# Six buffers for raw weights instead of four, and 42 places for activations instead of 46, in a two-layer hybrid decoder

## Chip, cores and metric

The kernel runs on one core of a Trainium2 chip. Its time is that of one execution on the device, in microseconds (us), and the median of several runs counts. TensorE (PE) does the matmuls, VectorE (DVE), ScalarE (ACT) and GpSimd (POOL) the work on elements, and SyncE (SP) issues most transfers (DMAs) from HBM to the on-chip memory.

## What is computed

Two layers of a decoder over 256 tokens of width 1024, in float32. Each layer has a shift, scale and gate from a vector c (adaLN), an input projection, three token mixers side by side, a merge, an output projection with a norm, and a feed-forward part with a short convolution. Cut to that:

```python
for l in range(DEPTH):
    mod = jax.nn.silu(c) @ mod_w[l] + mod_b[l]
    sh1, sc1, gt1, sh2, sc2, gt2 = jnp.split(mod[:, None, :], 6, axis=-1)
    h = x * (1.0 + sc1) + sh1
    z = h @ w_in[l]                       # layer 1: 32 more columns
    xa, ga, q, k, v, zc, zgate = _split(z, IN_SPLITS)
    y_a = _rg_lru(_causal_dwconv(xa, ...), ...) * jax.nn.gelu(ga)       # branch A
    y_b = _dilated_attention(rope(q), rope(k), v)                       # branch B
    y_c, v_first = _rwkv7_branch(_token_shift(zc, rwkv_mu[l]), ...)     # branch C
    g_a, g_b, g_c = jnp.split(jax.nn.sigmoid(zgate), N_BRANCH, axis=-1)
    merged = g_a * (y_a @ proj_a[l]) + g_b * (y_b @ proj_b[l]) + g_c * (y_c @ proj_c[l])
    x = _layer_norm(ALPHA * x + (1.0 + gt1) * (merged @ w_o[l]), ln1_w[l], ln1_b[l])
    h = x * (1.0 + sc2) + sh2
    u_g, u_v = jnp.split(_causal_dwconv(h @ ffn_up[l], ...), 2, axis=-1)
    x = _layer_norm(ALPHA * x + (1.0 + gt2) * ((jax.nn.silu(u_g) * u_v) @ ffn_down[l]), ln2_w[l], ln2_b[l])
```

## The kernel before

Channels lie on the partitions and tokens along the free axis. Every large product is made of three matmuls of a reduced-precision float32 type (fp32r): a weight is split in a high part `whi` (a rounded copy) and a low part `wlo` (the raw weight minus `whi`), an activation in the same way (`hh` and `hl` for the layer's input), and high times high, high times low and low times high are added up in PSUM. A weight item is one 128x1024 block, 512 KB, with 24 matmuls of 256 columns.

**The weights' path.** All weights pass in one list, `items`, in the order of their use. An item is loaded by SP to a raw buffer `w32` (the trace calls it `w`) from a ring of `NW` buffers. ACT or POOL then makes `whi` in two halves, and DVE or POOL `wlo` in two halves; `whi` and `wlo` have `WB` = 4 buffers each. The raw buffer is free again when the second `wlo` half is done. Between the weights stand the items of the modulation ("mods"): a column block of mod_w, which DVE multiplies by silu(c) and sums up, without PE; it needs a raw buffer and nothing else. In the feed-forward stage of the first layer the mods have a small ring of their own, of tiles `wc` in the activations' pool.

The loads are issued in this loop (`w_dma`), which the planner calls again and again; `wring` holds the items in the ring, and an item stands in `raw` until its `wlo` (or its reduction) has been written into the program:

```python
ring, room = (cring, NSC) if i in apart else (wring, NW)
old = ring[-room] if len(ring) >= room else None
if old in raw:
    return
```

So a load comes into SP's queue when the item `NW` places before it has been worked off by the program's order. On the chip the load waits until that work is done, and all loads behind it on SP wait with it.

**The start.** The first 16 mods make shift and scale of layer 0. Two of them, then the six weights of the first group (split to `ehi` and `elo`, in the activations' pool), and then the other 14 mods, with the four parts of x between them. Each pair of mods gives one of eight blocks of the layer's input: POOL and ACT make `h` and `hh`, DVE makes `hl`, and PE multiplies that block by all six weights (18 matmuls).

**What sets the order.** The order in which instructions stand on each engine is made when the program is built, by the class `Flow`. It keeps a clock per engine and for the loads, takes the dense matmuls as the main stream, and puts the steps of the branches, the mods and the splits between them by estimated times. It also chooses the engine of a split (`pick`, `pick_hi`). `NW` comes into it, since an item's arrival is worked out from the time at which its buffer is free. The engines then run their own queues in order and wait for each other by semaphores.

**The activations' pool.** Nearly all tiles of 128x512 float32 share one tag, `s2`, with `NS2` places of 2 KB per partition. A new tile takes a place whose tile has been released; the first write then waits for the last use of the old one. In branch C the recurrence over four chunks uses `KB`, `AL`, `AR`, `UV` and others of this pool, and writes the small tiles `R`, `UV` and `Y` on ACT step by step; branch A uses `rr`, `ii` and `tt`.

Of the kernel before, what the change touches and what calls it, by code (L numbers as in the profile page):

```python
# [50 lines left out]
DEBUG = None  # L51
WB = 4
TRACE = None
NW = 4
NG = 6
NSC = 2
NS2 = 46
NT1 = 21
HOLD = 0.3
BIAS_HI = 1.1  # L60
# [261 lines left out]
def hybrid_kernel(ctx: ExitStack, tc: tile.TileContext, x, c, positions, mod_w, w_in, w_qkv, w_vres, lru, lora, g2w,  # L322
# [22 lines left out]
    def s2(shape, name, dtype=F32):  # L345
        return sb.tile(shape, dtype, name=name, tag="s2", bufs=NS2)

# [25 lines left out]
    def fetch(dst, src, dep=0.0):  # L373

        nc.sync.dma_start(dst, src)
        n = dst.shape[0] / 128
        for d in dst.shape[1:]:
            n *= d
        fl.t["DMA"] = max(fl.t["DMA"], max(dep, fl.t["PE"]) + 1.1) + 0.00163 * n
        return fl.t["DMA"] + 1.0  # L380
# [20 lines left out]
    def w_dma():  # L401
        while state["dma"] < len(items):
            i = state["dma"]
            src, n, _, first = items[i]
            ring, room = (cring, NSC) if i in apart else (wring, NW)
            old = ring[-room] if len(ring) >= room else None
# [9 lines left out]
            else:  # L416
                raw[i] = wp.tile([128, 1024], F32, name="w32", bufs=NW)
                arrive[i] = fetch(raw[i][:, :n], src, dep)
# [1528 lines left out]
```

## Time and profile before

| | us |
|---|---|
| median of 3 runs | 1405.0 (1403.71 to 1406.58) |
| the profiled execution | 1404.2 |
| its span | 1402.5 |
| PE busy in it | 1322.6 |
| DVE busy | 1106.0 |
| ACT busy | 852.3 |
| POOL busy | 284.3 |

The span runs from the first to the last instruction of the profiled execution; the 1.7 us beside it are the ends of the launch. An engine's busy time counts its instructions, not its waits. Behind a row, the brackets name what ended the idle time before it. Matmuls are pipelined, so that their rows overlap.

### The profile page before, as it was taken

How to read it: one execution, taken by the hardware profiler on the slowest of the kernel's cores; microseconds unless marked ns; L12 is line 12 of the kernel's file. 1: busy time of each engine (PE TensorE's matmuls, PEld its weight loads, DVE VectorE, ACT ScalarE, POOL GpSimd, SP SyncE). 2: the span in 40 equal slices, each digit the busy share in tenths (PEclk: the TensorE clock that was granted, in tenths of full speed). 3: DMA queues.
4: the chain of work that ended last, by engine and by line, in shares of the span. 5: the costliest groups of instructions: out<-in, count | busy, mean ns of one | idle time of the engine just before them, and what ended most of it. 6: DMA issues, size and time to landing. Idle time of an engine off the chain costs nothing.

```text
span 1402.5 us, 32614 instructions
## 1 busy us (share of the span) xinstructions
PE 1322.6 (94%) x12798; PEld 1250.0 (89%) x12798; DVE 1106.0 (79%) x2547; ACT 852.3 (61%) x1755; POOL 284.3 (20%) x459
## 2 busy tenths in 40 slices
PE   4889999988999999999999999999999999999996
PEld 3789888887899999999999998988889899999996
DVE  7798778788668779999968748787788687799954
ACT  3546686666775557665457666755868454667643
POOL 2304141213200031110040321523205000510001
PEclk9999999989999999999999999999999999999998
DMA  8745435334447646778945443462435546267662
GB/s 307 247 148 181 129 95 189 117 123 136 152 144 248 209 166 209 243 256 293 328 159 181 137 127 111 150 212 92 152 107 191 181 150 226 94 226 240 195 188 66
DMA packets 77613, 249.21 MB, mean 178 GB/s; under 512 B 8754, under 2 KB 12082, under 8 KB 77460
## 3 DMA queue, kind: packets, MB, share of 16 engines
q1 hardware_dynamic: 76660, 244.62, 53.1%
q0 software_dynamic: 800, 2.52, 0.5%
q8 instruction: 100, 1.64, 0.5%
q14 instruction: 53, 0.43, 0.1%
HBM read 243.96 MB, written 3.15 MB: 176 GB/s over the span
## 4 chain that ended last, share of the span: by engine, by line
PE 58%; DVE 23%; ACT 9%; DMA 6%; issue 4%; POOL 0%; SPq 0%; DVEq 0%; ACTq 0%; POOLq 0%
PE mm L270 43%; PE aux L270 8%; DVE wlo L270 7%; PE faux L270 6%; DMA w<-in_w_in_dram 2%; DVE w L270 2%; ACT whi L270 2%; DVE u L270 2%; DVE xc L270 1%; DVE wc L270 1%; DVE BK L270 1%; DMA w<-in_w_up_dram 1%; DMA w<-in_mod_w_dram 1%; ACT L270 1%; DVE sq L270 1%
## 5 line engine op out<-in xcount | busy, mean ns | idle before, releaser
L270 PE MATMUL mm<-hh,whi 128*128 128x256 f32 x1696 | 499.5, 294 | 0.0
L270 ACT ACTIVATE whi<-w 128x512 fp32r<-128x512 f32 (+1 forms) x652 | 373.4, 617 | 200.4 <-PE mm L270 61.2
L270 PE MATMUL mm<-hh,wlo 128*128 128x256 f32 x1696 | 482.3, 284 | 7.3 <-DVE wlo L270 7.1
L270 PE MATMUL mm<-hl,whi 128*128 128x256 f32 x1696 | 480.9, 284 | 0.0
L270 DVE TENSOR_TENSOR wlo<-w,whi 128x512 fp32r<-128x512 f32 (+1 forms) x630 | 414.9, 695 | 50.4 <-ACT whi L270 47.2
L270 PEld LDWEIGHTS mm<-hh,whi 128*128 128x128 f32 x1696 | 321.4, 190 | 12.3 <-issue 4.3
L270 PEld LDWEIGHTS mm<-hh,wlo 128*128 128x128 f32 x1696 | 322.1, 190 | 10.9 <-DVE wlo L270 10.4
L270 PEld LDWEIGHTS mm<-hl,whi 128*128 128x128 f32 x1696 | 322.2, 190 | 1.1
L270 POOL TENSOR_TENSOR wlo<-w,whi 128x512 fp32r<-128x512 f32 x72 | 99.4, 1384 | 350.7 <-ACT whi L270 262.9
L270 POOL TENSOR_SCALAR whi<-w 128x512 fp32r<-128x512 f32 x50 | 33.5, 674 | 332.6 <-PE mm L270 258.6
L270 PE MATMUL mm<-fal,whi 128*128 128x256 f32 x352 | 98.8, 281 | 1.3 <-DVE fal L270 1.3
L270 PE MATMUL mm<-fah,wlo 128*128 128x256 f32 x352 | 99.1, 281 | 0.2 <-DVE wlo L270 0.2
L270 PE MATMUL mm<-fah,whi 128*128 128x256 f32 x352 | 99.0, 281 | 0.1
L270 DVE SCALAR_TENSOR_TENSOR u<-mm,par,u 128x255 f32<-128x255 f32 (+1 forms) x172 | 82.3, 479 | 14.0 <-ACT u L270 10.9
L270 PE MATMUL mm<-wlo,hh 128*128 128x256 f32 x288 | 82.4, 286 | 2.7 <-DVE wlo L270 2.7
L270 PE MATMUL mm<-whi,hh 128*128 128x256 f32 x288 | 83.9, 291 | 0.0
L270 PE MATMUL mm<-whi,hl 128*128 128x256 f32 x288 | 82.1, 285 | 0.0
L270 DVE SCALAR_TENSOR_TENSOR w<-w,s_bc 128x512 f32<-128x512 f32 x96 | 70.4, 756 | 0.5 <-DMA w<-in_mod_w_dram 0.4
L270 PEld LDWEIGHTS mm<-fal,whi 128*128 128x128 f32 x352 | 66.2, 188 | 1.6 <-DVE fal L270 1.5
L270 PEld LDWEIGHTS mm<-fah,wlo 128*128 128x128 f32 x352 | 66.2, 188 | 0.7 <-DVE wlo L270 0.6
L270 PEld LDWEIGHTS mm<-fah,whi 128*128 128x128 f32 x352 | 66.3, 188 | 0.3 <-ACT fah L270 0.3
L270 ACT ACTIVATE u<-mm,par 128x256 f32<-128x256 f32 x86 | 47.6, 556 | 28.7 <-PE mm L270 28.7
(446 smaller groups left out, 2728.8 us busy)
## 6 DMA issues: line engine op xcount, KB each, us to landing
w<-in_w_in_dram SPq DMA_DIRECT2D x132, 512.0 KB, 3.6
w<-in_w_up_dram SPq DMA_DIRECT2D x88, 512.0 KB, 4.4
w<-in_mod_w_dram SPq DMA_DIRECT2D x64, 512.0 KB, 4.5
w<-in_w_qkv_dram SPq DMA_DIRECT2D x36, 512.0 KB, 3.4
wc<-in_mod_w_dram SPq DMA_DIRECT2D x64, 256.0 KB, 5.0
w<-in_w_dn_dram SPq DMA_DIRECT2D x32, 512.0 KB, 4.6
w<-in_w_pa_dram SPq DMA_DIRECT2D x16, 512.0 KB, 4.3
w<-in_w_pc_dram SPq DMA_DIRECT2D x16, 512.0 KB, 3.8
```

The source lines that it names most:

```text
L270: r = f(*a, **k)
```

## The change

Two numbers change. The ring of raw weights gets two more buffers (2 x 4 KB per partition), and the activations' pool four places fewer (4 x 2 KB).

```diff
 WB = 4
 TRACE = None
-NW = 4
+NW = 6
 NG = 6
 NSC = 2
-NS2 = 46
+NS2 = 42
 NT1 = 21
```

Since the planner works with `NW`, the order on the engines is a new one from about 45 us on; ahead of that it is the same on every engine. The number of loads is unchanged.

On POOL, around 300 us, where PE multiplies the gate weights and the first weights of branch A. `itmp` and `VS` are steps of a small inverse in branch C; `w_3915` is the raw buffer of one weight item, and so on. Before:

```order
L270 TENSOR_TENSOR VS<-VS,itmp 128x7x2
L270 TENSOR_TENSOR itmp<-VS,N_3523 128x8
L270 TENSOR_TENSOR VS<-VS,itmp 128x8
L270 TENSOR_TENSOR wlo<-w_3915,whi 128x512
L270 TENSOR_SCALAR whi<-w_4182 128x512
L270 TENSOR_TENSOR wlo<-w_4182,whi 128x512 x2
```

Now:

```order
L270 TENSOR_TENSOR VS<-VS,itmp 128x7x2
L270 TENSOR_SCALAR whi<-w_3850 128x512
L270 TENSOR_TENSOR itmp<-VS,N_3544 128x8
L270 TENSOR_TENSOR VS<-VS,itmp 128x8
L270 TENSOR_SCALAR whi<-w_3850 128x512
L270 TENSOR_SCALAR whi<-w_3897 128x512
L270 TENSOR_TENSOR wlo<-w_3850,whi 128x512 x2
L270 TENSOR_TENSOR wlo<-w_3897,whi 128x512
L270 TENSOR_TENSOR wlo<-w_3972,whi 128x512
L270 TENSOR_TENSOR wlo<-w_3991,whi 128x512
L270 TENSOR_SCALAR whi<-w_4033 128x512
L270 TENSOR_TENSOR wlo<-w_3991,whi 128x512
```

On POOL stand now four halves of `whi` and seven of `wlo` (the last of them one row below these) for the items 3850 to 4033.

On ACT, around 956 us (layer 1), where branch C's recurrence of one pair of heads and branch A run side by side. `D_`, `N` and `VS` belong to the next pair of heads. Before:

```order
L270 ACTIVATE UV_11967<-aux 64x128
L270 ACTIVATE rr<-faux,h_ba_824 128x256
L270 ACTIVATE ii<-faux,h_bx_826 128x256
L270 ACTIVATE tt<-rr,sp_1119 128x256
L270 ACTIVATE Y<-aux 128x2x64
L270 ACTIVATE xc<-mm,par_84 128x256
L270 ACTIVATE whi<-w_12968 128x512
L270 ACTIVATE R<-aux 128x128
L270 ACTIVATE D__13221<-AL_13117 32x256
L270 ACTIVATE D__13221<-AL_13118 32x256
L270 ACTIVATE N_13230<-NP,pf 128x256
L270 ACTIVATE VS<-eye_153 128x128
```

Now:

```order
L270 ACTIVATE UV_11972<-aux 64x128
L270 ACTIVATE D__13200<-AL_13074 32x256
L270 ACTIVATE D__13200<-AL_13075 32x256
L270 ACTIVATE N_13209<-NP,pf 128x256
L270 ACTIVATE VS<-eye_153 128x128
L270 ACTIVATE rr<-faux,h_ba_854 128x256
L270 ACTIVATE ii<-faux,h_bx_856 128x256
L270 ACTIVATE tt<-rr,sp_1233 128x256
L270 ACTIVATE Y<-aux 128x2x64
L270 ACTIVATE xc<-mm,par_84 128x256
L270 ACTIVATE whi<-w_12863 128x512 x2
L270 ACTIVATE R<-aux 128x128
```

Branch A's `rr`, `ii` and `tt` have moved behind the next pair's `D_`, `N` and `VS`. With 42 places `ii` and `tt` take those of the pair `KB_12313` and `KB_12314`, two operands of the recurrence.

## Rows read from the trace of the kernel before

**Rows 1.** The page, parts 1 and 2: busy us (share) xinstructions; granted clock in tenths.

```profile
PE 1322.6 (94%) x12798; PEld 1250.0 (89%) x12798; DVE 1106.0 (79%) x2547; ACT 852.3 (61%) x1755; POOL 284.3 (20%) x459
...
PEclk9999999989999999999999999999999999999998
```

**Rows 2.** Stretches: us, busy PE, PEld, DVE, ACT, POOL (instructions); clock, DMA share, GB/s.

```profile
0.00:45.00 45.00, 20.74 (x114) 17.03 (x115) 34.99 (x93) 13.78 (x23) 9.94 (x22) 1.00 0.89 318
45.00:112.00 67.00, 59.36 (x452) 55.32 (x453) 57.23 (x184) 41.59 (x82) 16.84 (x32) 0.92 0.51 167
210.00:350.00 140.00, 126.48 (x1490) 115.80 (x1490) 113.92 (x244) 88.49 (x195) 33.54 (x62) 0.94 0.42 140
```

**Rows 3.** The chain that ended last, one step: start us, us, engine, instructions.

```profile
407.09 50.37 PE mm L270 x426
```

**Rows 4.** PE's waits in the whole run: us in total, times, longest us.

```profile
PE mm L270 <- DVE hl L270: 17.4, 5, 12.2
PE mm L270 <- DVE wlo L270: 9.9, 14, 3.2
```

**Rows 5.** SP's queue in the start, by the timeline: start us, us.

```profile
2.86 10.55 SPq L375 DMA_DIRECT2D w<-in_w_in_dram  x6
```

**Rows 6.** DVE in the first 46 us: two waits, and the first mod (timeline).

```profile
DVE w L270 <- DMA w<-in_mod_w_dram: 4.1, 7, 0.9
DVE elo L270 <- ACT ehi L270: 2.9, 4, 1.5
...
7.05 1.28 DVE L270 CUSTOM_DVE_ANT_0 w<-w,s_bc,modb 128x1024 f32<-128x1024 f32 x1 [0.93 <-DMA w<-in_mod_w_dram]
```

**Rows 7.** DMA, 0 to 42 us in 40 slices; loads to landing; a stretch as rows 2.

```profile
GB/s 0 2 127 195 291 417 417 410 425 417 320 332 164 285 281 289 226 378 412 421 373 300 316 316 359 258 341 404 425 390 328 328 224 275 417 394 339 254 285 324
...
w<-in_mod_w_dram SPq DMA_DIRECT2D x16, 512.0 KB, 5.4
...
28.80:45.80 17.00, 11.89 (x93) 11.07 (x93) 14.14 (x33) 3.21 (x6) 3.39 (x5) 1.00 0.95 354
```

**Rows 8.** PE's waits for `wlo`, and ACT's loads before two of them (timeline).

```profile
79.37 0.39 PE L270 MATMUL mm<-wlo,hh 128*128 128x256 f32 x1 [0.69 <-DVE wlo L270]
88.19 0.39 PE L270 MATMUL mm<-wlo,hh 128*128 128x256 f32 x1 [1.97 <-DVE wlo L270]
1253.65 0.39 PE L270 MATMUL mm<-hh,wlo 128*128 128x256 f32 x1 [1.64 <-DVE wlo L270]
...
78.08 1.15 ACT L270 ACTIVATE whi<-w 128x512 fp32r<-128x512 f32 x2 [1.02 <-DMA w<-in_w_qkv_dram]
1249.29 1.15 ACT L270 ACTIVATE whi<-w 128x512 fp32r<-128x512 f32 x2 [1.35 <-DMA w<-in_w_up_dram]
```

**Rows 9.** Branch A's `tt` and the last reads of `KB` and `AL` (timeline).

```profile
956.40 0.59 ACT L270 ACTIVATE tt<-rr,sp 128x256 f32<-128x256 f32 x1
956.52 0.46 PE L270 MATMUL aux<-UV,KB 128*64 128x64 f32 x8
961.64 0.28 PE L270 MATMUL aux<-UV,AL 64*64 64x64 f32 x2
```

**Rows 10.** Around 303 us: PE, DVE and POOL (timeline), and a stretch as rows 2.

```profile
306.19 0.58 PE L270 MATMUL mm<-hh,wlo 128*128 128x256 f32 x1 [3.23 <-DVE wlo L270]
301.13 1.78 DVE L270 SCALAR_TENSOR_TENSOR w<-w,s_bc 128x512 f32<-128x512 f32 x1
302.84 0.68 DVE L270 SCALAR_TENSOR_TENSOR w<-w,s_bc 128x512 f32<-128x512 f32 x1
301.06 1.31 POOL L270 TENSOR_TENSOR wlo<-w,whi 128x512 fp32r<-128x512 f32 x1 [14.96 <-ACT whi L270]
305.30:312.10 6.80, 5.91 (x85) 5.62 (x86) 6.55 (x16) 3.50 (x8) 0.00 (x0) 0.50 0.39 134
```

**Rows 11.** The page, part 5: POOL's splits, busy, mean ns, idle before.

```profile
L270 POOL TENSOR_TENSOR wlo<-w,whi 128x512 fp32r<-128x512 f32 x72 | 99.4, 1384 | 350.7 <-ACT whi L270 262.9
L270 POOL TENSOR_SCALAR whi<-w 128x512 fp32r<-128x512 f32 x50 | 33.5, 674 | 332.6 <-PE mm L270 258.6
```

## Prediction

> **What bounds the kernel now.** I read the page's engine table and slices first: TensorE (PE) is busy 94% of the span at a granted clock near full, so only PE's gaps and its half-clock stretches can be won [rows 1]. The busy times by stage tell where the gaps are: 24 of PE's 80 idle us lie in the first 45 us, 7.6 in the next 67, 13.5 between 210 and 350 [rows 2]. Where PE is fed it runs unbroken, 426 matmuls in 50.4 us, 0.118 us each; one weight item is 24 of them, 2.83 us [rows 3]. PE's list of waits tells for whom it stands: 17.4 us in all for `hl`, the low half of the first layer's input, all in the first 45 us, and 9.9 us in 14 waits for `wlo`, the low half of a weight [rows 4]. Only these two lie behind the raw buffers. The rest of the gaps are the serial steps of the recurrence (branch C) and the norms, which no raw buffer feeds.
>
> In the first 45 us the chain is: load, VectorE's (DVE) reduction of a modulation column, `hl`, PE. The DMA issues show the ring of four: once it is full the issuing queue stands until a buffer is free, so that six weights are spread over 10.55 us [rows 5]. DVE waits meanwhile: 4.1 us for loads of mods in seven waits (0.9 of it before the first load can be there) and 2.9 us for `ehi`, whose ScalarE (ACT) step waits for a weight's load [rows 6].
>
> **The change, term by term.** The sum is made against the profiled execution, 1404.2 us; the median of the runs shown, 1405.0, is 0.8 above it, and I add that at the end.
>
> *Start.* The items, their order and their instructions up to about 45 us are the same; only the buffer that each load waits for is two items older. Upper end: all of DVE's waits of [rows 6] but the very first go, 3.2 + 2.9 = 6.1 us. A round of one buffer is 5.4 us to landing [rows 7] and 1.4 us of reduction, 6.8 us; four buffers give an item each 1.7 us, six each 1.13 us, while DVE itself needs 1.54 us per mod (1.28 [rows 6], 0.08 to read the sum out, and half of a 0.34 us `hl`). So with six DVE sets the pace. Lower end: the DMA engines. From 28.8 to 45.8 us they were busy 0.95 at 354 GB/s [rows 7], which would be 373 GB/s when never idle. The single us from 10 to 16 show 320, 332, 164, 285, 281, 289 and 226 GB/s, mean 271, although 410 to 425 went through in the us 5 to 9 [rows 7]; filled up to 373, these seven us give 1.9 us, the stretch from 18 to 28.8 (mean 345) 0.8, the rest 0.9: 3.6 us. If the engines have nothing to give past the last 5%, 0.9. I take 4.0, near the 3.6, since DVE's pace (1.18 MB per pair of mods with its part of `x`, in 3.08 us, 383 GB/s) is just above what 373 feeds. PE then waits for `hl` less by as much; the steps behind it start from `hl` too and move along.
>
> The Trainium skill, page "DMA: Bandwidth & Descriptors", section Specifications, gives some 358 GB/s as the limit of HBM for one core, and that speaks against this term. By it the start would win 2.3 us (1.7, 0.4 and 0.2 in the three stretches) and the time would come to 1401. The trace has 410 to 425 GB/s in five us on end, so I don't take it as a ceiling.
>
> *Weights later on.* PE's waits for `wlo` whose ACT step waited for a load: 1.64 us at 1253.65, where ACT had stood 1.35 us for a load of w_up, and 0.69 us at 79.37 behind 1.02 us for a load of w_qkv [rows 8]. A load that is issued two items (5.7 us of PE) earlier is there. That is 2.3 us. Lower end 0 (the planner's order is new at both places), upper end 4.7: of the 9.9 us all but the 3.2 and 2.0 before which DVE, not a load, was late [rows 8, 10]. What is in it beyond 2.3 are ten small waits with no load just ahead of them. I take 2.3, the two with one.
>
> *The activations' pool, 42 places.* At 956.4 us branch A's `tt` is written, and counting tiles from first write to last read in the trace it is the 43rd in use; `NP` at 963.7 is one again. In the new order `ii` and `tt` get the places of the `KB` pair (the order of ACT there is shown above). Of before, `KB` was read last by matmuls from 956.52 for 0.46 us; the next tiles to be released there are the `AL`, read until 961.9 [rows 9]. So ACT is held 0.6 us, or 5.5 us if `AL` is what it waits for. I take 0.6, because `KB` stands there by name. Queued behind it on ACT are a `Y`, an `R` and the next `whi`; PE's recurrence waits for `R`, so nothing hides a long hold. At all other times 42 at most are in use.
>
> *The new order.* The planner is told that loads arrive earlier and puts about a third of the rows elsewhere. The amounts stay: the same matmuls, `wlo` 632 on DVE and 70 on GpSimd (POOL) for 630 and 72, `whi` 648 on ACT and 54 on POOL for 652 and 50, and two more table loads on ACT, 1.28 us each, beside an engine that is 61% busy. I take 0. What one place can do is seen at 303 us: PE stood 3.23 us for a `wlo` that DVE had put behind a mod and parts of the recurrence, and then ran 6.8 us at a clock of 0.50, the level of 1.2 GHz for 2.4 [rows 10], which costs 3.4 us more. One such place is 6.6 us either way.
>
> *Sum:* 1404.2 - 4.0 - 2.3 + 0.6 = 1398.5, as a median 1399.3; **1399 us**. Its own range, with the ends of the first three terms but a short hold: 1395 to 1402.
>
> **Rivals.** A measurement of this kernel can tell about 0.2% (2.8 us) from no change.
>
> *N, nothing.* More loads in flight only wait longer, since the engines that carry them are 95% busy already [rows 7]. Then the start wins 0.9, the weights 0, the pool costs 0.6: 1404. For it: that share. Against it: the holes in the GB/s of the us 10 to 16, which are no want of bandwidth.
>
> *B, a larger gain.* The wait at 303 us goes, because POOL takes the split of the weights there, as its new order shows: 1399 - 6.6 = 1392. For it: DVE is freed of seven halves of 0.69 us. Against it: see S.
>
> *S, slower.* At the same place POOL now has four `whi` and seven `wlo` halves nearly in a row, where before it had one `wlo`, after 14.96 us without work [rows 10]. One takes it 0.67 and 1.38 us [rows 11], together 12.3 us, for weights that PE uses up in 3.5 x 2.83 = 9.9 us: PE would be 2.4 us short. And DVE is slowed beside it: the half mod at 301.13 took 1.78 us with POOL's `wlo` beside it, the next one, free of POOL, 0.68 [rows 10], 1.1 us more; ten such meetings are 11 us, of which DVE's idle share (26 of 140 us, [rows 2]) covers 2. With 9 us on the path: 1408. It decides once DVE's delay there exceeds the gain of start and weights together, 6 us. The Trainium skill, page "SBUF — State Buffer", section "SBUF: two separate sides", says that a two-input DVE instruction and a POOL instruction take a shared port in turn, each for its whole length; by it every one of the ten would meet, and the time would be these 1408. The trace shows such a meeting at 301.13.
>
> **How the numbers follow.** Forecast 0.46, B 0.12, N 0.22, S 0.20 (with it the long hold of the pool, which would end near 1404 to 1408). Faster by over 0.2%: 0.46 + 0.12 = 0.58. Within 0.2%: 0.22. Slower: 0.20. The range runs from B's end to a little above S, 1391 to 1410; what lies outside is a second place like 303 us in one direction.
>
> **What would show it.** Start: the six loads of weights go out within 8 us and not 10.55, DVE's waits for mods fall from 4.1 below 2 us, PE's for `hl` from 17.4 to 13 or less, and its idle time in the first 45 us from 24 to 20. If loads take over 7 us to land and DVE still waits 4 us, N is right. Weights: no wait of PE for `wlo` above 1 us with a load behind it. Pool: ACT's row before `ii` near 950 us has a wait for PE, under 1 us or about 5. B or S: PE's idle time and POOL's busy time between 285 and 320 us, and DVE's mean for `wlo`, 0.695 us now. The forecast is wrong if the start wins its 4 us and the sum doesn't show them: then the order took them back, in new waits of PE between 210 and 350 or 930 and 1110 us.

## The result, and the profile after

The changed kernel takes 1383.4 us (median of 4, 1382.6 to 1384.9) against 1405.8 for the kernel before, a ratio of 0.9845 with an interval of 0.9817 to 0.9873. That is 22 us faster, where 6 were forecast, and outside the range. The profiled spans differ by 20.6 us. The page of after, parts 1 and 2 (as [rows 1]):

```profile
span 1381.9 us, 32627 instructions
...
PE 1308.9 (95%) x12798; PEld 1240.6 (90%) x12798; DVE 1099.3 (80%) x2549; ACT 852.7 (62%) x1753; POOL 285.3 (21%) x461
...
PEclk9999999999999999999999999999999999999998
```

PE's idle time fell from 79.9 to 73.0 us, so two thirds of the gain are not idle time. Of the 13.7 us that went out of PE's *busy* time, 8.5 are matmuls that ran at half clock before (shown below); 3.3 are matmuls at full clock that were stretched behind short waits (the next one begins later than the usual 0.118 us), and the rest is small. The start is the place to see the first part. SP's queue and PE's last wait for `hl` in the timeline, the waits of DVE (first 46 us) and PE, and the DMA rate in 40 slices of 1.05 us (as [rows 4 to 7]):

```profile
2.84 7.00 SPq L375 DMA_DIRECT2D w<-in_w_in_dram  x6
...
39.52 0.38 PE L270 MATMUL mm<-hl,ehi 128*128 128x256 f32 x1 [0.51 <-DVE hl L270]
```

```profile
DVE w L270 <- DMA w<-in_mod_w_dram: 1.6, 3, 0.9
...
DVE elo L270 <- ACT ehi L270: 0.9, 2, 0.6
...
PE mm L270 <- DVE hl L270: 12.5, 5, 9.4
```

```profile
GB/s 0 4 148 201 319 410 421 421 421 417 421 410 406 410 410 414 396 404 410 417 406 398 412 412 421 406 410 400 406 416 402 414 398 417 406 421 390 402 417 406
...
w<-in_mod_w_dram SPq DMA_DIRECT2D x17, 512.0 KB, 6.9
```

All holes of the DMA rate are filled, at 390 to 421 GB/s for 36 us on end. A load takes 6.9 us to land instead of 5.4, because more are under way at once (an estimate: 6.9 us at 410 GB/s are 2.8 MB, between five and six loads; 5.4 us at 345 GB/s are 1.9 MB, between three and four). Even so DVE waits only 1.6 us for mods, where it had waited 4.1. The Trainium skill, page "DMA: Bandwidth & Descriptors", section Specifications, has some 358 GB/s as one core's share of HBM; the measured rate, in this program on one core, is above it throughout.

Three stretches of before and two of after, columns as [rows 2]; the number to read is the granted clock, third from the end (0.50 is 1.2 GHz, 1.00 is 2.4):

```profile
45.80:49.20 3.40, 3.40 (x18) 3.40 (x18) 0.70 (x2) 1.43 (x3) 2.29 (x4) 0.51 0.72 245
66.30:69.70 3.40, 3.40 (x18) 3.40 (x17) 3.23 (x17) 2.61 (x6) 0.75 (x2) 0.50 0.76 271
93.60:97.00 3.40, 3.40 (x18) 3.08 (x20) 3.26 (x11) 1.61 (x4) 0.00 (x0) 0.50 0.34 90
```

```profile
41.70:45.10 3.40, 3.40 (x28) 2.89 (x27) 1.10 (x3) 1.83 (x5) 3.32 (x7) 1.00 1.01 394
73.00:76.40 3.40, 3.40 (x18) 3.40 (x17) 3.37 (x9) 1.69 (x5) 0.00 (x0) 0.50 0.52 158
```

Before, PE had waited 0.92, 1.35, 0.92 and 1.91 us for `hl` between 32 and 45 us, and ran the next 3.4 us at half clock; after, it waited 0.67, 1.38, 0.49 and 0.51, and the clock stayed at full (first row of after). Of the four kernels here with four buffers in the start three have such a stretch by 46 us (at 45.8 in before, 38.7 in e2 and 46.3 in e5 below), while e10 keeps the full clock there and has 6.8 us of half clock from 63 us on; of the seven with five or six buffers none has one before 57 us. In the whole span half-clock stretches cost 24.0 us before and 15.5 after (length times what the clock lacked).

ACT's waits for loads, over the whole run, of before and of after (us, times, longest):

```profile
ACT whi L270 <- DMA w<-in_w_up_dram: 50.8, 40, 3.0
...
ACT whi L270 <- DMA w<-in_w_dn_dram: 15.4, 14, 3.0
...
ACT whi L270 <- DMA w<-in_w_in_dram: 12.9, 11, 2.5
```

```profile
ACT ehi L270 <- DMA w<-in_w_in_dram: 2.8, 1, 2.8
```

Before, ACT stood 96.6 us for loads in all; after, once, for the first weight of the program.

**Where the lead arises.** The table gives by how much the same dense matmul (counted from the start) begins earlier than in the kernel before; four of the experiments below stand beside it. Times are those of before. Each column is one profiled execution: that of e1 is 3.0 us below the median of its kernel, that of e2 1.6 above.

| before, us | after | e1 buffers alone | e2 order alone | e5 four in the start | e6 six in the start |
|---|---|---|---|---|---|
| 58, start done | 8.1 | 8.1 | 1.0 | -1.1 | 8.0 |
| 558, in layer 0's up-projection | 9.8 | 6.0 | -1.6 | 1.7 | 7.9 |
| 671, in its down-projection | 14.0 | 8.1 | -1.2 | 5.9 | 6.6 |
| 930, layer 1 | 13.3 | 7.4 | -4.9 | 5.3 | 4.1 |
| 1110 | 14.5 | 8.5 | -5.4 | 6.6 | 4.9 |
| 1138 | 18.3 | 12.4 | -1.6 | 10.3 | 8.8 |
| 1267 | 19.9 | 13.9 | -5.4 | 12.0 | 7.0 |
| 1390, end | 20.6 | 14.5 | -5.0 | 12.3 | 7.5 |

### The profile page after: what moved, and what is told of

Read it like the earlier page. It is cut to its first block, busy times and chain, and to the rows that moved or that the text cites. A ratio compares the mean times of both kernels' runs of the same rounds, so it can differ in the third digit from the quotient of the medians.

```text
span 1381.9 us, 32627 instructions
## 1 busy us (share of the span) xinstructions
PE 1308.9 (95%) x12798; PEld 1240.6 (90%) x12798; DVE 1099.3 (80%) x2549; ACT 852.7 (62%) x1753; POOL 285.3 (21%) x461
## 4 chain that ended last, share of the span: by engine, by line
PE 70%; DVE 17%; ACT 7%; issue 3%; DMA 2%; POOL 0%; SPq 0%; DVEq 0%; ACTq 0%; POOLq 0%
PE mm L270 54%; PE aux L270 9%; PE faux L270 7%; DVE wlo L270 4%; DVE w L270 1%; ACT whi L270 1%; DVE BK L270 1%; DVE xc L270 1%; ACT L270 1%; DVE wc L270 1%; DMA w<-in_mod_w_dram 1%; DMA wc<-in_mod_w_dram 1%; DVE X L270 1%; DVE u L270 1%; ACT rr L270 1%
## 5 line engine op out<-in xcount | busy, mean ns | idle before, releaser
L270 DVE TENSOR_TENSOR wlo<-w,whi 128x512 fp32r<-128x512 f32 (+1 forms) x632 | 414.8, 691 | 45.8 <-ACT whi L270 45.0
L270 POOL TENSOR_TENSOR wlo<-w,whi 128x512 fp32r<-128x512 f32 x70 | 97.0, 1390 | 234.9 <-ACT whi L270 226.7
L270 POOL TENSOR_SCALAR whi<-w 128x512 fp32r<-128x512 f32 x54 | 37.9, 703 | 405.9 <-PE mm L270 342.1
L270 DVE SCALAR_TENSOR_TENSOR u<-mm,par,u 128x255 f32<-128x255 f32 (+1 forms) x172 | 82.2, 479 | 13.2 <-ACT u L270 10.0
```

The lines of the kernel that those rows point to most:

```text
L270: r = f(*a, **k)
```

## Experiments

The first theory was that the buffers themselves do it (B), its rival that the planner's new order does (O).

**Buffers without the order.** The planner reckons with four buffers for the items before number 300, while six exist. Up to about 915 us every engine has the order of before.

```diff
-            ring, room = (cring, NSC) if i in apart else (wring, NW)
+            ring, room = (cring, NSC) if i in apart else (wring, 4 if i < 300 else NW)
```

> Six raw buffers and 42 places, but the planner reckons with four for all items before number 300, so that every engine has the order of the kernel before up to about 935 us (behind that a third order). Theory B (the buffers do it: loads are there earlier, ACT no longer stands for them): ahead of the kernel before by 8 us at 58 us, by 11 at 560 us and by 14 at 930 us, as the changed kernel is, and some 1386 to 1392 us in all. Theory O (the new order does it): only the start's 8 us, nothing in the feed-forward stage, and about 1397 us.

It took 1392.8 us, ratio 0.9892 (0.9867 to 0.9917). Neither theory has it: the start's 8.1 us are there in full, of the 4.2 us between 558 and 671 us 2.1, but the branches of layer 0 took 2.1 back. At 930 us it is 7.4 us ahead and not 14. Behind that the order is not a third one, as expected, but row by row that of after, and it gains as much there as after does: 7.1 us against 7.3. So e1 tests the old order with six buffers up to there only.

**The order without the buffers.** The planner's ring and the real one are separated: `arrive` is worked out with a ring of PLAN items, and the load goes out when the buffer NW items back is free. (The parts of `x` may go out a little earlier on SP by it; the same holds for the next three kernels with PLAN.)

```diff
+NW = 4
+PLAN = 6
...
-            ring, room = (cring, NSC) if i in apart else (wring, NW)
+            ring, room = (cring, NSC) if i in apart else (wring, PLAN)
...
+                old = wring2[-NW] if len(wring2) >= NW else None
+                if old in raw:
+                    return
+                raw[i] = wp.tile([128, 1024], F32, name="w32", bufs=NW)
+                nc.sync.dma_start(raw[i][:, :n], src)
```

> Four raw buffers and 46 places, but the planner reckons with six: PE, DVE, ACT and POOL have exactly the order of the changed kernel, and a load goes out when the fourth buffer before it is free. Theory B: no better than the kernel before, 1402 to 1410 us, ACT standing for loads again in the feed-forward stage (20 us between 558 and 637). Theory O: 1390 to 1396 us, the gain without the start's 8 us.

1407.6 us, ratio 0.9993 (0.9974 to 1.0011): nothing, as B says. ACT's waits show where the new order loses what it gains elsewhere: it puts `whi` where it reckons with a load that is not there. The long waits stand at 476 us (w_o, 4.7 us), 926 (w_in, 4.1), 1142 (w_pc, 4.4) and 1163 (w_o, 3.5), and the lead falls by 5, 4 and 4 us between 454 and 558, 671 and 930, 1138 and 1267 us. That the one makes the other is argued from these places.

```profile
ACT whi L271 <- DMA w<-in_w_up_dram: 52.1, 40, 3.2
...
ACT whi L271 <- DMA w<-in_w_o_dram: 8.2, 2, 4.7
...
ACT whi L271 <- DMA w<-in_w_pc_dram: 4.4, 1, 4.4
```

At 930 us the new order is worth 13.3 - 7.4 = 5.9 us with six buffers and -4.9 with four, by single executions. Over whole runs it is worth some 6.6 us with six (the ratios 0.9892 and 0.9845) and nothing with four (0.9993). The two parts of the change are not a sum.

**Another count.** Five buffers and 44 places; and six with a planner that reckons with eight, with the edit of e2 and `PLAN = 8`. Both were meant to give other orders.

```diff
-NW = 4
+NW = 5
...
-NS2 = 46
+NS2 = 44
```

> Five raw buffers and 44 places, planner told so. Theory B: the first extra buffer takes most of the waits for loads, so more than half of the 22 us: 1386 to 1394 us. Theory O: the order is a new draw; anything between 1385 and 1410 us, with no relation to the number of buffers.

> Six raw buffers and 42 places, but the planner reckons with eight, which gives another order on all engines; a load goes out when the sixth buffer before it is free. Theory B: within 5 us of the changed kernel, 1380 to 1389 us. Theory O: the good order is lost, over 1392 us.

Both took 1385.0 us (0.9839, 0.9813 to 0.9864, and 0.9833, 0.9808 to 0.9858). But they are not other orders: with the planner at eight, PE, DVE, ACT and POOL have row by row the order of after, against what was expected, and with five they have it too, but for two neighbouring rows of ACT near 901 us. So e4 is after measured again, and neither tests whether the order was a lucky draw. Together with e2 they show something else, the buffers alone at one and the same order: four 1407.6 us, five 1385.0, six 1383.4 (e4 1385.0). The first extra buffer brings nearly all. With five, ACT's largest wait for loads behind the start is

```profile
ACT whi L270 <- DMA w<-in_w_up_dram: 3.1, 4, 1.7
```

**One step down.** Three buffers and 46 places.

> Three raw buffers and 46 places, the planner told so. A step down the same curve: with four ACT waits 90 us for loads and the time is 1405, with five 6 us and 1385. Theory B: with three ACT's waits are far above 90 us, PE waits for wlo in the dense stages too, and the time is over 1450 us. If four were near the knee of the curve on this side too: under 1425 us.

1458.2 us, ratio 1.0383 (1.0362 to 1.0404), with 205 us of ACT's waits for loads. Two of its rows:

```profile
ACT whi L270 <- DMA w<-in_w_up_dram: 65.7, 54, 3.3
...
ACT whi L270 <- DMA w<-in_w_in_dram: 55.5, 32, 6.6
```

The curve from three to six, with the order that the planner makes for each, is 1458, 1405, 1385, 1383 us, with waits of ACT for loads of 205, 97, 9 and 3 us.

**Start and rest.** In the order of after, all four engines row by row, the first 24 items go through four of the six buffers, or through six with four from there on.

```diff
+                k = len(wring2)
+                room = 4 if k < 24 else NW
+                old = wring2[-room] if k >= room and k not in (24, 25) else None
...
+                if k >= 24 and k % NW < 2:
+                    raw[i] = wp.tile([128, 1024], F32, name="w32", tag="w32b", bufs=NW - 4)
+                else:
+                    raw[i] = wp.tile([128, 1024], F32, name="w32", bufs=4)
```

> Exactly the order of the changed kernel on PE, DVE, ACT and POOL, six raw buffers and 42 places, but the first 24 items go through four of the six buffers. If the start is worth 8 us and the rest 14: PE's waits for hl are back at 17 us, a half-clock stretch is back near 46 us, 7 to 9 us behind the changed kernel at 58 us and in the end, 1390 to 1393 us. If the branches behind the start have slack for a late start: under 1387 us.

> The mirror of it: the order of the changed kernel, six raw buffers for the first 24 items, four from there on. If start and rest add up: the order alone with four buffers (1407.6) less 8 us, 1398 to 1401 us, and ACT's waits for loads of up-projection weights at about 52 us as with four. If the start's buffers bring the later gain too, by the planner's lead: under 1390 us.

1392.9 us (0.9922, 0.9905 to 0.9939) and 1396.6 us (0.9949, 0.9931 to 0.9966). The first is where it was expected, the second 1.4 us below its band. Against after the start is worth 9.5 us by the medians (8.3 by the spans), the rest 13.1 (13.1); the two make 22.6 of the 24.2 us between e2 and after by the medians (25.4 against 20.8 by the ratios), so they add up within some 4 us. With four in the start the half clock is back at 46.3 us and PE's waits for `hl` are 19.1 us. With four in the rest nothing is lost up to 454 us (10.6 us ahead, as after); 7.4 us are gone by 671 us and 5.7 more behind that, with ACT's waits back:

```profile
ACT whi L271 <- DMA w<-in_w_up_dram: 52.0, 40, 3.5
```

**The places.** Five buffers with 42 places instead of 44, the order being the same row by row.

> Five raw buffers with 42 places instead of 44: what fewer places cost alone. If places cost nothing, as the trace of the changed kernel says (no wait of ACT ahead of ii): within 0.1% of 1385.0 us. If a hold of 0.6 to 5.5 us exists as the prediction had it: 1385.6 to 1390.5 us, with a wait for PE ahead of a write of a new tile.

1386.4 us, ratio 0.987 (0.985 to 0.989), against 0.9839 for 44 places. The time decides nothing: 1386.4 lies within 0.1% of 1385.0 and also in the band given for a hold. The traces do: ACT's rows at `ii` and `tt` are the same with 44 and 42 places, without a wait, and in the changed kernel itself the writes of `ii` and `tt` have none ahead of them either. So there is no hold for a place there:

```profile
946.57 0.29 ACT L270 ACTIVATE VS<-eye 128x128 f32<-128x128 f32 x1
946.77 0.46 ACT L270 ACTIVATE rr<-faux,h_ba 128x256 f32<-128x256 f32 x1
947.13 0.46 ACT L270 ACTIVATE ii<-faux,h_bx 128x256 f32<-128x256 f32 x1
947.48 0.59 ACT L270 ACTIVATE tt<-rr,sp 128x256 f32<-128x256 f32 x1
```

**The feed-forward stage.** The same 624 matmuls of the up-projection take 78.9 us before, 74.9 after, and 78.9 in e2, which has the order of after and four buffers (columns as [rows 2]). The window begins just behind a loss of 1.1 us: from the up-projection's first matmul at 524 us, where the lead was 10.9, to the down-projection's last the changed kernel gains 3.1 us and not 4.

```profile
558.00:636.90 78.90, 76.81 (x625) 74.93 (x625) 77.70 (x169) 49.07 (x103) 11.50 (x8) 1.00 0.73 246
```

```profile
548.20:623.10 74.90, 74.60 (x626) 74.16 (x625) 73.94 (x167) 51.26 (x105) 13.20 (x10) 1.00 0.74 259
```

```profile
559.60:638.50 78.90, 76.58 (x627) 74.75 (x626) 77.15 (x164) 48.61 (x102) 15.30 (x11) 1.00 0.73 247
```

DVE is busy over 98% in before and after, though ACT waits 20.3 us for loads in the former and not at all in the latter. Its rows for a weight half or a mod half are 0.68 us, but eight of before (ten of after) are longer, each beside a `wlo` on POOL. One of before, one of after (timeline):

```profile
598.62 1.65 POOL L270 TENSOR_TENSOR wlo<-w,whi 128x512 fp32r<-128x512 f32 x1 [4.74 <-ACT whi L270]
...
599.05 1.76 DVE L270 SCALAR_TENSOR_TENSOR wc<-wc,s_bc 128x512 f32<-128x512 f32 x1
```

```profile
613.67 1.29 POOL L270 TENSOR_TENSOR wlo<-w,whi 128x512 fp32r<-128x512 f32 x1 [7.24 <-ACT whi L270]
614.26 1.26 DVE L270 SCALAR_TENSOR_TENSOR wc<-wc,s_bc 128x512 f32<-128x512 f32 x1
```

All eighteen DVE rows end 0.55 us behind the POOL row beside them, so DVE did nearly all of its 0.68 us of work after POOL had ended. The Trainium skill, page "SBUF — State Buffer", section "SBUF: two separate sides", has such a pair of instructions take a shared port in turn; these rows agree, and add that the price of a meeting is what is left of POOL's row when DVE arrives, less 0.13 us (0.2 to 1.1 us here). The excess over 0.683 us sums to 5.8 us in eight meetings before and 3.2 in ten after; in e2, with the order of after but four buffers, to 7.5 in eleven. So with later loads the meetings of one and the same order cost more. With the two halves that POOL took over (1.4 us) the 2.6 us make 4.0, as much as the whole difference. To test that (M) against ACT's waits for loads (L), all `wlo` halves of the stage were put on DVE, with six buffers and with four. Cut to the first of two such lines; `ffn` holds the stage's items:

```diff
-            eng = pick(m, dep)[0]
+            eng = V if i in ffn else pick(m, dep)[0]
```

> The changed kernel, but every wlo half of the first layer's feed-forward stage is made on DVE; PE's order is the same. The stretch of 624 matmuls that takes 74.9 us in the changed kernel holds ten halves on POOL: DVE gets 10 x 0.685 = 6.9 us more and loses the 3.2 us by which its rows were lengthened beside POOL. Theory M (DVE's rows and their meetings with POOL set this stage, loads do not): 78.6 us, and as long with four buffers as with six. Theory L (ACT's waits for loads set it): still about 4 us shorter than with four buffers. In all 1386 to 1389 us.

> The kernel before with the same edit. The stretch takes 78.9 us there, with eight halves on POOL: DVE gets 8 x 0.685 = 5.5 us more and loses the 5.8 us by which its rows were lengthened. Theory M: 78.6 us again, and the whole kernel unchanged at 1403 to 1406 us. Theory L: 82 us or more, and about 1409 us.

The stretches with POOL out of them, six and four buffers:

```profile
547.00:623.50 76.50, 75.86 (x626) 74.59 (x625) 75.56 (x173) 50.54 (x105) 0.00 (x0) 1.00 0.75 253
```

```profile
559.90:638.10 78.20, 76.47 (x626) 74.84 (x625) 75.79 (x174) 49.05 (x103) 0.00 (x0) 1.00 0.73 243
```

In all 1384.5 us (0.9852, 0.9832 to 0.9872) and 1402.4 us (0.9978, 0.9956 to 0.9999), both a little faster than either theory had it. With four buffers M has the stretch within 0.4 us. With six it is 2.1 us under M's figure, and six stays 1.7 us ahead of four at equal DVE time (75.6 and 75.8), where L asked for some 4. So neither theory has it alone: of the 4.0 us, some 1.7 are the loads, PE and DVE standing less behind ACT; the other 2.3 are POOL's share and its meetings with DVE. These are two single executions.

## Why the prediction was wrong

The direction and the start's mechanism were right, the size was not: two terms of the sum were too small, the weights later on (2.3 us taken, 13 measured) and the start (4.0 taken, 8 to 9.5 measured).

**Start: mechanism right, its consequence left out.** The six weights went out in 7.0 us (under 8 forecast), DVE's waits for mods fell to 1.6 (under 2), PE's for `hl` to 12.5 (13 or less), PE's idle time in the first 45 us to 19.3 (20). The term itself measured 4.9 us against 4.0 taken. But the lead at 58 us is 8.1, and four buffers in the start cost 8.3 of the span. The step that failed here is "PE then waits for `hl` less by as much; the steps behind it start from `hl` too and move along": with the shorter waits PE also had no half-clock stretch at 45.8 us, 1.7 us. The page showed that stretch, and the prediction priced such a stretch at 303 us but not here. The last 1.5 us are small gaps and stretched matmuls behind them. How much of the 8.1 is the one execution of before stays open: e10 begins like before, has no half clock at 46 us and is 2.8 us ahead of it at 58 us, but loses that by 66 us in its stretch from 63 us on. The lower end too rested on a wrong ceiling: 373 GB/s was worked out from a stretch with holes, and the engines have 410 to give.

**Weights later on: mis-sized, 2.3 against 13.** This is the step that failed most: "PE's waits for `wlo` whose ACT step waited for a load" were taken for all that a late load costs, and the "ten small waits with no load just ahead of them" were left out. No wait of PE for `wlo` has a load behind it any more, as forecast. But of the two waits that were named only that at 1253.65 us is gone. The one at 79.37 us, 0.69 before, is 2.80 after: ACT had made the last `whi` ahead of it by 68.8 us, but DVE came to this half of `wlo` only at 71.4, behind some twenty small steps, and a half-clock stretch follows at 73.0 us.

```profile
72.10 0.39 PE L270 MATMUL mm<-wlo,hh 128*128 128x256 f32 x1 [2.80 <-DVE wlo L270]
```

And the later buffers are worth 13 us in the order of after (e6). PE's waits for `wlo` show half of it, 12.1 us with four buffers behind the start and 5.7 with six (the rows of e6, then of after; before has 10.7 in an order that reckons with late loads):

```profile
PE mm L271 <- DVE wlo L271: 7.8, 15, 1.7
...
PE faux L271 <- DVE wlo L271: 4.3, 3, 1.9
```

```profile
PE mm L270 <- DVE wlo L270: 3.9, 3, 2.8
...
PE faux L270 <- DVE wlo L270: 1.8, 1, 1.8
```

ACT's waits, 96.6 us for loads, stand in no line of the prediction. What these waits cost passes through the order: DVE and POOL get `whi` later than the planner reckoned, and a late `wlo` collides with the next mod, as measured in the feed-forward stage, or stands behind a step of the recurrence, which is argued. Between 558 and 637 us, where nothing was priced, 4.0 us were won.

**The order: taken as 0.** With four buffers 0 is what the runs show (0.9993); with six the new order is worth some 6 us by 930 us. That it "puts about a third of the rows elsewhere" was read as a draw of either sign; here an order made for early loads was good when the loads were early. Whether another such order would be as good stays open, since the planner made the same one for five, six and eight buffers. One single place was a draw: at 1094.7 us PE stood 2.3 us for `DN` and then ran at half clock for 3.4 us, which costs 1.7 more, 4.0 together. The order of after does not have that stall, not even with four buffers (e2); e10, which keeps the order of before there, has it. In the table, where the leads swing until the branches are done, it is the 3.8 us from the row of 1110 to that of 1138. Its row, and the stretch around it:

```profile
1096.98 1.00 PE L270 MATMUL aux<-DN,Om 32*32 32x32 f32 x64 [2.33 <-DVE DN L270]
```

```profile
1094.00:1101.00 7.00, 4.67 (x144) 4.14 (x143) 5.61 (x11) 3.19 (x8) 1.26 (x1) 0.76 0.41 132
```

**The places: 0.6 taken, none found.** In after, the last matmuls that read `KB` ran from 944.24 us for 0.46, and ACT came to `ii` at 947.13, since `D_`, `N` and `VS` stand ahead of it from 944.08 on. The rows shown with the change have them ahead of `rr`, and the prediction still took the distance between write and read from the order of before.

**Rivals.** N fell with the DMA rate. B's place did not get better: around 303 us the wait for `wlo` went, but PE now stands 4.4 us for `X` of the recurrence and runs at half clock again, since a mod and two weight halves are ahead of it on DVE. PE's idle time between 285 and 320 us rose from 3.9 to 5.5 us, and POOL's busy time from 3.2 to 13.2 (the stretch of after, and DVE's and PE's rows of the timeline):

```profile
285.00:320.00 35.00, 29.49 (x384) 28.04 (x382) 29.64 (x59) 24.82 (x47) 13.18 (x13) 0.90 0.41 137
```

```profile
305.72 0.68 DVE L270 SCALAR_TENSOR_TENSOR w<-w,s_bc 128x512 f32<-128x512 f32 x1
...
308.49 1.73 PE L270 MATMUL aux<-X,AL 32*32 32x32 f32 x32 [4.43 <-DVE X L270]
```

So S had the place right and the price wrong: 1.6 us more idle time, not 9 (roughly, since the two stretches do not hold the same matmuls). A meeting of DVE and POOL cost 0.2 to 1.1 us in the feed-forward stage, where S took 1.1 each time. N's 1404 leaves out the 0.8 us that the sum adds for the median. DVE's mean for `wlo` over the run is 0.691 us, 0.695 before.

What stays open: where the half of the 13 us that PE's waits for `wlo` do not show was won outside the feed-forward stage; what the old order would do with six buffers behind 915 us; and how the 5.9 us of the order up to 930 us divide among its places, since in the branches the leads of two orders swing by 10 us and more and mean something only where the stages meet.

## What to carry to other kernels

Read who waits for loads on *every* engine, not only on the one that bounds the kernel: 97 us of ACT's waits were a sign of a ring that is one buffer short, though almost none of them stood directly before PE. Where a planner or a person orders the work by estimated arrivals, buffers and order have to be valued together: here the order alone was worth nothing, the buffers with the old order for two thirds of the program 14 of the 22 us. It pays to compare the orders themselves before two kernels are called two draws. And a wait that is removed should be priced with the half-clock stretch that follows it in the profile, as a chance and not for certain.

## What was not expected of the hardware

The same wait is not always followed by the half clock. The kernels with five buffers and 44 or 42 places have the same order, and in both PE waits 1.85 us for a `wlo` near 1122 us. Behind it one ran at full clock and the other at half (44 places, then 42):

```profile
1125.10:1128.50 3.40, 3.40 (x31) 3.40 (x30) 2.24 (x8) 0.00 (x0) 0.00 (x0) 1.00 0.78 288
```

```profile
1125.80:1129.20 3.40, 3.40 (x19) 3.40 (x18) 2.24 (x8) 0.00 (x0) 0.00 (x0) 0.51 0.81 282
```

The difference is 1.7 us, and a second such pair at 982 us gives as much again: more than the two places are worth, and a bound on what one trace can say about a change of a microsecond.
